# A hybrid encoder layer on one core: the feed-forward tiles lie 32 bytes further apart in SBUF

## The chip, the cores and the metric

The kernel runs on one NeuronCore of a Trainium2 chip. The metric is the device time of one execution in microseconds. Three executions of the kernel before took 3914.40, 3920.77 and 3924.82 us; the median, 3920.77 us, is the time before.

## The reference, cut to what matters

One layer: an input projection feeds a Hyena convolution and an RWKV-7 scan, their outputs are gated, joined and projected (`w_o`), normalised, and a SwiGLU feed-forward network follows. All data are float32; the sequence has 2048 rows of 1024 channels, the feed-forward network is 2816 wide.

```python
D_MODEL = 1024; SEQ = 2048
FFN_HIDDEN = ((8 * D_MODEL + 3 * 256 - 1) // (3 * 256)) * 256      # 2816
...
mix = (g_h * y_h + g_r * y_r) @ w_o
x = layer_norm(DN_ALPHA * x + mix, ln1_w, ln1_b)
ffn = (jax.nn.silu(x @ ffn_w_gate) * (x @ ffn_w_up)) @ ffn_w_down
return layer_norm(DN_ALPHA * x + ffn, ln2_w, ln2_b)
```

## The kernel before

Four stages follow one another in `build`: `project` (the input projection, with other work woven between its matmuls), `chain` and `hyena` (scan and convolution), `merge` (gates, `w_o`, first normalisation) and `ffn`. The first three take the span's first 2443 us or so, `ffn` the rest but its end.

**How a float32 product is made.** Every large operand is split into two tiles of type float32r: `hi`, a rounded copy that ScalarE casts (L196), and `lo`, what is left, which VectorE subtracts (L197). `mm3` (L199 to L203) then issues three matmuls, hi by hi (L201), and the two mixed ones (L202, L203), into one PSUM tile. In the feed-forward stage each has a moving operand of 512 columns and loads a new stationary operand of 128 columns (in a part of `merge` the moving operand has 256). The profile shows the load as an instruction of its own (PEld).

**The feed-forward stage.** `ffn` runs over two halves of 1024 tokens, and in each half over `NF` = 22 slices of 128 hidden channels. For each slice `weights` (L1803 to L1814) loads three pieces of 128 x 1024 (`fg`, `fu`, `fd`) into a raw tile and splits each into `fwh` and `fwl`, two buffers of each. For each of two blocks of 512 tokens the slice makes the gate `pg` and the up projection `pu` (8 x 3 matmuls each, stationary the weights, moving the transposed activations `fxh`, `fxl`), then `silu(pg) * pu`, split into the hidden tiles `hh` and `hl` (L1845). `down` multiplies those (stationary) with the `fd` tiles (moving) into `pd`, and VectorE adds `pd` to eight accumulators `acc0` to `acc7` (L1830). The down projection of one slice is put between the two blocks of the next, so that PE has work while ScalarE and VectorE finish the hidden tile. In all there are 2 x 22 x (96 + 48) = 6336 matmuls of 512 columns in the stage.

**Where the tiles lie.** Tiles come from pools; a pool sets its tags down one after the other, in the order in which they are first asked for, each at a multiple of 32 bytes. Beside `ffn`, the pool `mf` also serves `merge`: its 16 tiles `wo` (the split `w_o`, L1691) take the tags of the feed-forward weights and hidden tiles, so they lie at the same places. The first tile of `mf`, `leps` (L261), holds one constant but is 48 elements (192 bytes) wide. In the built program it starts at byte 83936 of a partition, and every tile of `mf` of 2 or 4 KB or more starts at a multiple of 256 plus 160. So do the activations of the first block (pool `xp1`) and the projection's weights (pool `wp`): **both operands of every float32r matmul of the kernel start at the same remainder, 160, modulo 256**, since the slices inside the tiles are whole multiples of 256 bytes. The raw tiles lie at remainders 96, 128 and 160.

**The order** of instructions follows the program text here, within each engine's queue; loads of weights are issued by SyncE, casts run on ScalarE, subtractions and sums on VectorE.

Of the kernel before, what the change touches and what calls it, by code (L numbers as in the profile page):

```python
# [188 lines left out]
class Layer:  # L189
# [38 lines left out]
    def build(self):  # L228
        tc, nc = self.tc, self.nc
        with tc.tile_pool(name="dr", bufs=1, space=DRAM) as dr, tc.tile_pool(name="keep", bufs=1, reuse_waits="tile") as keep:  # L230
            T = lambda n, s: dr.tile(s, F32, name=n)
            self.ident = self.load(keep, "c_ident")
            self.H3d = T("H3d", [P, 32, P])
            self.ud = T("ud", [27, P, L])
            self.gated = T("gated", [16, P, L])
            self.ABd = T("ABd", [2, NCH, P, HP, 256])
            self.Vd = T("Vd", [L, 512])
            self.gsd = T("gsd", [P, L])
            self.Yd = T("Yd", [NCH, P, 256])
            self.Hd = T("Hd", [2 * HT, 32, P, P])  # L240
            self.Nd, self.Wd = T("Nd", [2, P, 1024]), T("Wd", [2, P, 1024])
            self.yhd = T("yhd", [HT, P, L])
            self.bond = T("bond", [HP, P, L])
            self.yrd = T("yrd", [HP, P, L])
            self.x1d = T("x1d", [L, D])
            self.keep = keep

            self.Dk = keep.tile([P, 264], F32, name="Dk", tag="Dk")[:, 0:256].rearrange("p (d h c) -> p d h c", d=2, h=HP)
            with tc.tile_pool(name="xp1", bufs=1, reuse_waits="tile") as self.xp1, tc.tile_pool(name="fp", bufs=1, reuse_waits="tile") as self.fp:
                with tc.tile_pool(name="wp", bufs=1, reuse_waits="tile") as self.wp:  # L250
                    accp = tc.tile_pool(name="accp", bufs=2, space=PSUM, reuse_waits="tile")
                    self.accp = accp.__enter__()
                    self.cut, self.rush, self.stores = 1, 0, nc.scalar
                    self.project()
                    with tc.tile_pool(name="cm", bufs=1, reuse_waits="tile") as self.cm:
                        self.chain()
                        accp.__exit__(None, None, None)
                        self.hyena()
                    with tc.tile_pool(name="mf", bufs=1, reuse_waits="tile") as self.mf:

                        self.leps = self.mf.tile([P, 48], F32, name="leps")[:, 0:1]  # L261
                        for g in ("acc2", "acc3", "lw", "lb"):
                            self.mf.tile([P, D], F32, name=g, tag=g)
                        nc.vector.memset(self.leps, LN_EPS)
                        self.merge()
                        self.ffn()
# [1376 lines left out]
    def merge(self):  # L1643
        tc, nc, i, s = self.tc, self.nc, self.i, self.mf
        stt = nc.vector.scalar_tensor_tensor
        with tc.tile_pool(name="mgp", bufs=2, space=PSUM, reuse_waits="tile") as ps:
            ys = {"r": self.yr}
            wm = {"r": self.wr, "h": [s.tile([P, 8, 4, P], F32R, name=f"wh{n}", tag=f"fx{n}1") for n in "hl"]}
            for b in range(L // TB):
                tl = slice(TB * b, TB * b + TB)  # L1650
                rs = {}
                if b == 0:
                    rs = {dt: self.rs[dt // 4][:, dt % 4] for dt in range(7)}
                    y0, y2, w0 = self.early
                    self.branch_weights("h", 0, wm["h"], w0)
                    hl = [s.tile([P, 4, TB], F32R, name="y", tag=f"acc{2 + k}") for k in range(2)]
                    self.split(hl[0][:, 0:2], hl[1][:, 0:2], y0)
                    self.split(hl[0][:, 2], hl[1][:, 2], y2)
                    ys["h"] = [(hl[0][:, k], hl[1][:, k]) for k in range(3)] + [(self.yh[:, 0], self.yh[:, 1])]

                    def more(dt):
                        m = min(2, 8 - dt)
                        raw = self.wp.tile([P, 2, 4, P], F32, name="wr", tag="wl" if dt < 4 else "wh", bufs=2)[:, 0:m]
                        nc.sync.dma_start(raw, i["w_hy"][dt:dt + m].rearrange("c p k d -> p c k d"))
                        self.split(wm["h"][0][:, dt:dt + m], wm["h"][1][:, dt:dt + m], raw)

                    more(1)
                    more(3)
                mh, ml = ([s.tile([P, 4, TB], F32R, name="mx", tag=f"acc{4 + 2 * v + k}") for k in range(2)] for v in range(2))
                for dt in range(8):  # L1670
                    g = self.h512().rearrange("p (a b) -> p a b", b=TB)
                    part = [(0, "h", g[:, 0])]
                    if b == 0 and dt in (1, 3):
                        more(4 + dt)
                    if dt not in rs:
                        rs[dt] = g[:, 1]
                        part.insert(0, (1, "r", g[:, 1]))
                    for j, n, v in part:
                        self.gate(v, j, dt, tl)
                        p = ps.tile([P, TB], F32, name="pm", tag="pm" + n)  # L1680
                        self.joined(p, wm[n], ys[n], dt)
                        self.merged(v, v, p)
                    hi, lo = mh[dt // 4][:, dt % 4], ml[dt // 4][:, dt % 4]
                    o = g[:, 0]
                    nc.vector.tensor_tensor(out=o, in0=o, in1=rs[dt], op=ALU.add)
                    nc.scalar.activation(hi, o, AF.Copy, scale=0.5)
                    stt(out=lo, in0=o, scalar=0.5, in1=hi.bitcast(F32), op0=ALU.mult, op1=ALU.subtract)
                if b == 0:
                    self.ln_consts("ln1")
                    tags = [f"fw{v}{n}" for k in range(2) for n in ("fg", "fu", "fd") for v in "hl"] + ["hh", "hl"] * 2  # L1690
                    wo = [s.tile([P, D], F32R, name="wo", tag=g, bufs=2) for g in tags]  # L1691
                    for k in range(KT):
                        raw = self.raw()
                        nc.sync.dma_start(raw, i["w_o"][:, k])
                        self.split(wo[2 * k], wo[2 * k + 1], raw)
                if b + 1 < L // TB:
                    ys = {n: self.branch(n, b + 1) for n in "rh"}
                last = b == L // TB - 1
                if last:
                    self.x0 = []  # L1700
                    beside = self.turn_block(ps, ("pmr", "pmh"), 0, 0, self.x0)
                    next(beside)
                for t in range(2):
                    tk = 2 * b + t
                    tl = slice(P * t, P * t + P)
                    x = s.tile([P, D], F32, name="fx", tag="fx", bufs=FX)
                    nc.sync.dma_start(x, i["x"][P * tk:P * tk + P])
                    p = ps.tile([P, 2, 512], F32, name="po", tag="po")
                    for k in range(KT):
                        if last and t == 1:  # L1710
                            next(beside, None)
                        for n in range(2):
                            cl = slice(512 * n, 512 * n + 512)
                            self.mm3(p[:, n], mh[k // 4][:, k % 4, tl], ml[k // 4][:, k % 4, tl],
                                     wo[2 * k][:, cl], wo[2 * k + 1][:, cl], k == 0, k == KT - 1)
                    stt(out=x, in0=x, scalar=ALPHA, in1=p.rearrange("p a b -> p (a b)"), op0=ALU.mult, op1=ALU.add)
                    self.norm(s, x)
                    nc.sync.dma_start(self.x1d[P * tk:P * tk + P], x)
# [73 lines left out]
    def ffn(self):  # L1792
# [3 lines left out]
        with tc.tile_pool(name="ffp", bufs=2, space=PSUM, reuse_waits="tile") as ps:  # L1796
# [7 lines left out]
            def weights(f, spare=False):  # L1804
                w = {}
                for n in ("fg", "fu", "fd"):
                    raw = self.raw()
                    nc.sync.dma_start(raw, i[n][f].rearrange("p k c -> p (k c)") if n != "fd" else i[n][f])
                    t = "fu" if spare and n == "fd" else n
                    hi = s.tile([P, D], F32R, name="fwh", tag="fwh" + t, bufs=2)  # L1810
                    lo = s.tile([P, D], F32R, name="fwl", tag="fwl" + t, bufs=2)
                    self.split(hi, lo, raw)
                    w[n] = hi, lo
                return w  # L1814
# [24 lines left out]
            for half in range(2):  # L1839
                acc, nxt, pend = [], [], []  # L1840
                for f in range(NF):
                    if f:
                        w = weights(f, half and f == NF - 1)

                    hh, hl = (s.tile([P, 1024], F32R, name="h" + v, tag=f"fw{v}fg" if half and f == NF - 1 else "h" + v, bufs=2) for v in "hl")  # L1845
                    ready = f > 0 and not (half and f >= NF - 2)
                    for b in range(2):
                        xh, xl = xs[b]
# [44 lines left out]
```

## Time and profile before

| | |
|---|---|
| time before (median of 3; lowest, highest) | 3920.77 us (3914.40, 3924.82) |
| the profiled execution: its own time | 3916.3 us |
| its span, first to last instruction | 3913.2 us |
| around the span | 3.1 us |
| mean granted TensorE clock | 0.989 |
| busy: PE, PEld, DVE, ACT, POOL | 96%, 77%, 60%, 35%, 3% |

How to read it: PE is the matmul side of TensorE, PEld its weight loads (they run beside matmuls), DVE is VectorE, ACT ScalarE, POOL GpSimd, SP SyncE. The duration of one matmul (some 390 ns) is its way through the array, and successive matmuls overlap; what counts for the time is the distance from one matmul's start to the next one's, the **pitch**, which is read from a timeline or from a count of matmuls in a window. "fp32r" in a row is the split type.

### The profile page before, as it was taken

What the parts mean: (1) busy time and instruction counts of PE and PEld (TensorE: products, weight loads), DVE (VectorE), ACT (ScalarE), POOL (GpSimd) and SP (SyncE); (2) the same over time, 40 slices, a digit from 0 to 9 for tenths busy, and PEclk for the clock granted to TensorE, in tenths of its full rate; (3) what the DMA queues carried; (4) which work ended last, traced back from release to release, by engine and by line L of the source; (5) the groups of instructions that cost most, each with busy time, mean ns of one, the idle gap of its engine ahead of it and who ended that gap; (6) DMA issues with size and microseconds to landing.
All of it is one profiled execution on the core that took longest, in us unless ns stands there. A gap on an engine that the chain in (4) does not pass through costs nothing. (4 is left out here: it accounts for less than half of the span.)

```text
span 3913.2 us, 62098 instructions
## 1 busy us (share of the span) xinstructions
PE 3775.7 (96%) x24808; PEld 3001.6 (77%) x24808; DVE 2345.5 (60%) x3734; ACT 1366.3 (35%) x2583; POOL 127.8 (3%) x203
## 2 busy tenths in 40 slices
PE   8999999999999998999998999999999999999998
PEld 6776657788787887766657998788888878888887
DVE  4466885666667775667776556444444474444444
ACT  3355663333335655444444323211111141111113
POOL 0000001111010110000000000000000000000000
PEclk9999999999999999999999999999999999999999
DMA  4556878677777777756656334311111141111111
GB/s 138 175 167 175 219 216 254 194 227 212 208 221 229 219 221 224 203 151 175 172 153 196 117 115 137 134 49 49 49 49 49 49 146 59 49 49 49 49 49 43
DMA packets 430229, 551.48 MB, mean 141 GB/s; under 512 B 138019, under 2 KB 305451, under 8 KB 427187
## 3 DMA queue, kind: packets, MB, share of 16 engines
q1 hardware_dynamic: 364405, 459.37, 39.7%
q10 hardware_dynamic: 54528, 54.59, 4.6%
q0 software_dynamic: 11008, 33.57, 3.2%
q8 instruction: 195, 3.19, 0.4%
q14 instruction: 93, 0.76, 0.1%
HBM read 385.76 MB, written 144.70 MB: 136 GB/s over the span
## 5 line engine op out<-in xcount | busy, mean ns | idle before, releaser
L201 PE MATMUL acc<-xh,wh 128*128 128x512 f32 x1376 | 573.1, 417 | 11.7 <-ACT xh L196 8.8
L202 PE MATMUL acc<-xl,wh 128*128 128x512 f32 x1376 | 543.5, 395 | 3.8 <-DVE xl L197 3.8
L203 PE MATMUL acc<-xh,wl 128*128 128x512 f32 x1376 | 542.7, 394 | 0.5 <-DVE wl L197 0.5
L1830 DVE TENSOR_TENSOR acc<-pd,acc 128x1024 f32<-128x1024 f32 x320 | 387.4, 1221 | 68.6 <-PE pd L203 63.3
L196 ACT CAST fwh<-raw 128x1024 fp32r<-128x1024 f32 x132 | 138.9, 1052 | 702.3 <-PE pg L202 485.2
L201 PEld LDWEIGHTS acc<-xh,wh 128*128 128x128 f32 x1376 | 261.3, 190 | 120.2 <-issue 47.1
L1858 DVE TENSOR_TENSOR h<-pu,sg 128x512 f32<-128x512 f32 x88 | 60.9, 692 | 477.7 <-PE pu L203 470.6
L202 PEld LDWEIGHTS acc<-xl,wh 128*128 128x128 f32 x1376 | 261.9, 190 | 60.0 <-DVE xl L197 6.2
L203 PEld LDWEIGHTS acc<-xh,wl 128*128 128x128 f32 x1376 | 261.7, 190 | 58.6 <-DVE wl L197 1.7
L201 PE MATMUL pd<-fwh,hh 128*128 128x512 f32 x704 | 275.3, 391 | 1.6 <-DVE acc L1828 1.2
L201 PE MATMUL pu<-fxh,fwh 128*128 128x512 f32 x704 | 274.6, 390 | 0.4 <-ACT fxh L1744 0.4
L201 PE MATMUL pg<-fxh,fwh 128*128 128x512 f32 x704 | 274.7, 390 | 0.0
L203 PE MATMUL pd<-fwh,hl 128*128 128x512 f32 x704 | 274.6, 390 | 0.0
L202 PE MATMUL pd<-fwl,hh 128*128 128x512 f32 x704 | 274.6, 390 | 0.0
L203 PE MATMUL pg<-fxh,fwl 128*128 128x512 f32 x704 | 274.4, 390 | 0.0
L202 PE MATMUL pg<-fxl,fwh 128*128 128x512 f32 x704 | 274.4, 390 | 0.0
L203 PE MATMUL pu<-fxh,fwl 128*128 128x512 f32 x704 | 274.1, 389 | 0.0
L202 PE MATMUL pu<-fxl,fwh 128*128 128x512 f32 x704 | 274.0, 389 | 0.0
L197 DVE TENSOR_TENSOR fwl<-raw,fwh 128x1024 fp32r<-128x1024 f32 x132 | 161.2, 1222 | 167.3 <-ACT fwh L196 163.3
L197 DVE TENSOR_TENSOR wl<-wraw,wh 128x512 fp32r<-128x512 f32 (+1 forms) x217 | 169.5, 791 | 135.7 <-ACT wh L196 129.0
L196 ACT CAST wh<-wraw 128x512 fp32r<-128x512 f32 (+1 forms) x217 | 150.7, 703 | 223.8 <-PE acc L202 192.2
L201 PEld LDWEIGHTS pd<-fwh,hh 128*128 128x128 f32 x704 | 132.0, 188 | 40.3 <-DVE acc L1830 12.3
(298 smaller groups left out, 7195.5 us busy)
## 6 DMA issues: line engine op xcount, KB each, us to landing
wraw<-in_w_in SPq DMA_DIRECT2D x130, 512.0 KB
ABp<-ABd SPq DMA_DIRECT2D x64, 512.0 KB
raw<-in_fg SPq DMA_DIRECT2D x44, 512.0 KB
raw<-in_fu SPq DMA_DIRECT2D x44, 512.0 KB
raw<-in_fd SPq DMA_DIRECT2D x44, 512.0 KB
ud<-ev ACTq DMA_DIRECT2D x84, 256.0 KB
ABd<-AB SPq DMA_DIRECT2D x32, 512.0 KB
rg<-in_c_win POOLq DMA_DIRECT2D x64, 256.0 KB, 4.0
```

The costliest lines, as they stand in the source:

```text
L196: nc.scalar.copy(hi, src)
L197: nc.vector.tensor_tensor(out=lo, in0=src, in1=hi.bitcast(F32), op=ALU.subtract)
L201: mm(ps, ah, bh, start=start, stop=False)
L202: mm(ps, ah, bl, start=False, stop=False)
L203: mm(ps, al, bh, start=False, stop=stop)
L1830: tt(out=acc[t], in0=pf, in1=acc[t], op=ALU.add)
L1858: tt(out=h, in0=put, in1=sg, op=ALU.mult)
```

## The change

It makes five tile declarations wider, and uses the same number of elements of each as before: `leps` from 48 to 56 elements, and the tiles of the split `w_o`, of the split feed-forward weights and of the hidden activations from 1024 to 1032 elements, of which the first 1024 are used. So each such tile ends 32 bytes later, and everything behind it in the pool moves on.

```diff
-                        self.leps = self.mf.tile([P, 48], F32, name="leps")[:, 0:1]
+                        self.leps = self.mf.tile([P, 56], F32, name="leps")[:, 0:1]
...
-                    wo = [s.tile([P, D], F32R, name="wo", tag=g, bufs=2) for g in tags]
+                    wo = [s.tile([P, D + 8], F32R, name="wo", tag=g, bufs=2)[:, 0:D] for g in tags]
...
-                    hi = s.tile([P, D], F32R, name="fwh", tag="fwh" + t, bufs=2)
-                    lo = s.tile([P, D], F32R, name="fwl", tag="fwl" + t, bufs=2)
+                    hi = s.tile([P, D + 8], F32R, name="fwh", tag="fwh" + t, bufs=2)[:, 0:D]
+                    lo = s.tile([P, D + 8], F32R, name="fwl", tag="fwl" + t, bufs=2)[:, 0:D]
...
-                    hh, hl = (s.tile([P, 1024], F32R, name="h" + v, tag=f"fw{v}fg" if half and f == NF - 1 else "h" + v, bufs=2) for v in "hl")
+                    hh, hl = (s.tile([P, D + 8], F32R, name="h" + v, tag=f"fw{v}fg" if half and f == NF - 1 else "h" + v, bufs=2)[:, 0:1024] for v in "hl")
```

The instructions are the same in number, operation, operands and order on every engine, and each waits for the same. What differs is the start address of 676 tiles of `mf` (a buffer that is used again is counted each time). Start addresses modulo 256, from the two built programs:

| tiles | before | after |
|---|---|---|
| activations of the first block, `fxh`, `fxl` (pool `xp1`) | 160 | 160 |
| activations of the second block; weights `whh`, `whl` of `merge` | 160 | 192 |
| `acc2` to `acc7`, `h`, `lw`, `lb`, `mx` | 160 | 192 |
| `fwh` of `fg` and of `fd`, two buffers | 160, 160 | 192, 224 |
| `fwl` of `fg` and of `fd` | 160, 160 | 0, 32 |
| `fwh` of `fu` | 160, 160 | 64, 96 |
| `fwl` of `fu` | 160, 160 | 128, 160 |
| hidden `hh` | 160, 160 | 64, 96 |
| hidden `hl` | 160, 160 | 128, 160 |
| `wo`, 16 tiles | 160 each | each of the eight remainders twice |
| `fx`, `junk` | 160 | 192 |

The raw tiles, `acc0`, `acc1` and everything ahead of `merge` stay where they are. The last tile of the pool ends at byte 228288 of a partition (227744 before).

## The prediction

> **What bounds the kernel now.** I read the page first: its head, the busy shares and the chain that ended last.
>
> ```profile
> span 3913.2 us, 62098 instructions
> PE 3775.7 (96%) x24808; PEld 3001.6 (77%) x24808; DVE 2345.5 (60%) x3734; ACT 1366.3 (35%) x2583; POOL 127.8 (3%) x203
> PE 45%; DVE 2%; DMA 1%; ACT 1%; issue 0%; SPq 0%; DVEq 0%; ACTq 0%
> ```
>
> PE is busy 96% of the span, and no other engine holds more than 2% of the chain. The change touches `merge` and `ffn`, so I then asked for windows of that part: all engines over the stage, then PE alone in two quiet pieces and behind the last matmul.
>
> ```profile
> 2440.00:3902.00 1462.00, 1454.83 (x6438) 1194.45 (x6437) 724.85 (x732) 297.40 (x413) 0.00 (x0) 1.00 0.18 62
> ...
> 2700.00:3100.00 400.00, 400.00 (x1764) 1.00 0.15 49
> 3300.00:3700.00 400.00, 400.00 (x1763) 1.00 0.15 50
> 3902.00:3913.20 11.20, 0.00 (x0) 0.70 0.35 140
> ```
>
> In the first row the columns behind the length are busy time and count of PE, PEld, DVE, ACT and POOL, then granted clock, DMA share and GB/s; the others show PE alone. DVE works half of the stage (725 of 1462 us), ACT a fifth, DMA 18%. PE has no idle time in 2700 to 3100 and in 3300 to 3700: 400 us / 1763.5 matmuls is a pitch of **226.8 ns**. The stage's 6336 matmuls of 512 columns at that pitch are 1437 us; the other 25 us of the 1462 are transposes, the start and two changeovers. The stage is therefore a count times a pitch, and a change of addresses alone can matter only through the pitch, through 11 us of tail, or by making another engine late.
>
> **What the pitch is made of.** The timeline of `merge`, where the same product runs with 256 columns, gives a second point.
>
> ```profile
> 2087.94 0.28 PE L202 MATMUL pm<-y,whh 128*128 128x256 f32 x1
> ...
> 2088.90 0.28 PE L201 MATMUL pm<-y,whh 128*128 128x256 f32 x1
> ```
>
> Eight matmuls lie between these starts (by line: 202, 203, 201, and so on): 0.96 / 8 = 120 ns. So 256 columns more cost 226.8 - 120 = 106.8 ns, or 0.417 ns a column; 512 columns are 213.5 ns, and some **13 ns a matmul** are left over at either width. This rest is the only thing in the pitch that a collision of addresses could be hiding in. A float32 product, which reads its columns at half that speed, shows less of it:
>
> ```profile
> 1615.40 0.59 PE L1309 MATMUL pz<-Vf,Mc 128*128 128x512 f32 x1
> 1615.83 1.02 PE L1350 MATMUL pq<-rg,Mc 128*128 128x512 f32 x2
> 1616.68 1.02 PE L1351 MATMUL pq<-rg,Mc 128*128 128x512 f32 x2
> ```
>
> From 1615.40 to 1616.68 are three pitches of 0.427 us, and 1024 times 0.417 ns is the same 427 ns: a rest of some 2 ns at most. These operands start at remainders 224 and 96, not at one remainder. So either the rest of 13 ns belongs to the fast type, or it belongs to equal remainders; the profile does not hold the pair that would settle it, a float32r product with unequal ones.
>
> **The change, part by part.** *Instructions*: none is added, removed or moved, no operand and no wait differs, so nothing stands behind a new wait and no queue is passed. That term is 0. *DMA*: the raw tiles that the weights land in stay where they are: 0.
>
> *Matmuls*: 6336 in `ffn` and 768 of `w_o` in `merge`, 7104 in all, get a new pair of remainders or a new place; some 744 products of `merge` move with both operands by the same 32 bytes. Each nanosecond of mean pitch is worth 7.1 us, so 0.3% of the time (11.8 us, about what a measurement of this kernel can tell from no change) is 1.7 ns a matmul. Three observations speak for 0.
>
> First, the two streams do not keep step. A load of 64 stationary columns takes 140 ns, one of 128 takes 188:
>
> ```profile
> L847 PEld LDWEIGHTS pY<-SV,rg 128*64 128x64 f32 x1024 | 54.7, 140 | 0.0
> L201 PEld LDWEIGHTS pg<-fxh,fwh 128*128 128x128 f32 x704 | 132.5, 188 | 28.0 <-DVE fxl L1745 0.4
> ```
>
> That is 48 / 64 = 0.75 ns a column against 0.417 for the moving operand. While a load reads its 512 bytes (128 x 0.75 = 96 ns), the stream passes 96 / 0.417 = 230 columns or 920 bytes, and the distance between the two runs through 408 bytes, more than a whole turn of 256. Whatever remainder they start at, they meet at nearly every other. A start offset moves the moment of a meeting, not the number of meetings.
>
> Second, a shift in time is a shift of that distance, and the trace has some. Usually the next load starts with the matmul; at a changeover it comes late:
>
> ```profile
> 2487.69 0.39 PE L201 MATMUL pg<-fxh,fwh 128*128 128x512 f32 x1
> 2487.91 0.40 PE L201 MATMUL pd<-fwh,hh 128*128 128x512 f32 x1
> 2488.15 0.39 PE L202 MATMUL pd<-fwl,hh 128*128 128x512 f32 x1
> 2488.38 0.40 PE L203 MATMUL pd<-fwh,hl 128*128 128x512 f32 x1
> ...
> 2487.46 0.19 PEld L201 LDWEIGHTS pg<-fxh,fwh 128*128 128x128 f32 x1
> 2487.80 0.19 PEld L201 LDWEIGHTS pd<-fwh,hh 128*128 128x128 f32 x1
> ```
>
> The matmul of 2487.69 has a load beside it that starts 0.11 us late. By then the stream is some 110 / 0.417 = 264 columns or 1056 bytes in (the rows' 10 ns are 96 bytes, so which remainder the two then stand at is not known, only that it is hardly the same one as in step). Its pitch is 0.22 us, as ever. (The next pitch, 0.24, follows a load that came in time.)
>
> Third, the one pass in which the trace does have equal and unequal remainders is the transpose through the identity (remainder 128), with `y` at 128, `BK` at 64, `co` at 224, `fx` at 160:
>
> ```profile
> 1198.41 0.38 PE L882 MATMUL pgt<-k_c_ident,y 128*128 128x128 f32 x2
> 716.57 0.60 PE L790 MATMUL pT<-k_c_ident,BK 128*128 128x128 f32 x4
> 1579.45 0.93 PE L1282 MATMUL ph<-k_c_ident,co 128*128 128x128 f32 x7
> 3158.17 0.93 PE L1742 MATMUL pxt<-k_c_ident,fx 128*128 128x128 f32 x7
> ...
> L1742 PE MATMUL pxt<-k_c_ident,fx 128*128 128x128 f32 x128 | 18.6, 274 | 4.8 <-DMA fx<-x1d 2.3 <-DVE fxl L1745 1.9 <-DVE fwl L197 0.6
> ```
>
> With the 0.274 us of one (last row) taken off, the pitch is 0.106 for the equal pair (one step), and 0.109, 0.109 and 0.109 for the unequal ones: the same within the rows' rounding of 10 ns a step. These run at half speed, so they are weaker witnesses than the second.
>
> Bounds for this term: at best the rest falls from 13 ns to the 2 ns of the float32 rows, -11 ns or -78 us; at worst all pitches become the 0.235 us that the two behind 2487.91 show (0.47 / 2), +8 ns or +57 us. I take **0**, to which the three observations lie nearest, and keep both ends.
>
> *VectorE and ScalarE*: their tiles move as well. Both wait for PE in this stage:
>
> ```profile
> ACT fwh L196 <- PE pg L202: 485.2, 41, 13.3
> DVE h L1858 <- PE pu L203: 470.6, 85, 8.8
> ...
> L197 DVE TENSOR_TENSOR hl<-h,hh 128x512 fp32r<-128x512 f32 x88 | 60.1, 683 | 2.7 <-ACT hh L196 2.7
> L911 DVE TENSOR_TENSOR yo<-yo,bn 128x512 f32<-128x512 f32 x16 | 11.0, 689 | 3.4 <-ACT yo L893 3.3
> L485 DVE TENSOR_TENSOR sh<-u 128x512 f32<-128x512 f32 x60 | 40.7, 687 | 34.0 <-DMA u<-ud 33.7
> ```
>
> One VectorE form takes 683 ns on tiles at 160, 689 on tiles at 0 and 687 on tiles at other remainders: a spread of 1%, on an engine that is idle half of the time. PE's matmuls hide it; without that cover 1% of 725 us would be 7 us. In the tail, where nothing hides it, 1% of 11.2 us is 0.1 us. Does PE feel the others? In the two pieces of 400 us with DVE and ACT working beside it the pitch is as short as anywhere: 0. Sum: **0 us**.
>
> **What the pages say.** The Trainium skill, "SBUF — State Buffer", section "🔬 SBUF: two separate sides", has it that engines hinder one another only at the port shared by VectorE and GpSimd, which leaves addresses out; the sum by it is 0, and POOL's 0.00 us in the stage agrees. "TensorE: Matmul & The Clock Gate" of the Trainium skill, section "Back-to-back issue gap", gives N/2.4 + 2.5 ns, 216 ns at 512 columns. The 226.8 of this trace are 11 more, so by that page there would be 7104 x 11 = 78 us to win if equal remainders were what holds the fast type back; its section "Step-by-step: what each phase is for" speaks against that, since loads and streams have read ports of their own.
>
> **The rivals.** *Faster*: the rest of 13 ns is a collision of load and stream at equal remainders, and the change takes it away in 22 of 24 pairs of feed-forward tiles (of eight each in gate, up and down projection, two stay equal: 192 with 192 and 160 with 160). For it: the float32 rows, with unequal remainders and a rest of 2 ns. Against: the late load, the drift. In full 3920.8 - 78 x 22/24 = 3849 us; in part, anything from 3909.
>
> *Slower*: equal remainders are what keeps load and stream apart, since a load starts with its matmul and the same 32-byte slots are then read in a fixed order; unequal ones put both on one slot, and each such pair pays the 8 ns of the 0.235 us pitch. For it: a kernel with nearly all pitches at 226.8 and all remainders equal leaves room for only this. Against: the same drift. In full 3920.8 + 57 x 22/24 = 3973 us. It decides from 1.7 ns of mean pitch, when one pair in five pays.
>
> *It doesn't do what it says*: the addresses of the built program differ as stated, so this is out.
>
> **How the numbers follow.** The profiled execution took 3916.3 us, 3.1 of them around the span; with a sum of 0 it stays 3916.3. It lies 4.5 us under the median of the runs, 3920.8, which is what I forecast. Chances: no change 0.70, faster 0.17, slower 0.13; within 0.3% is 3909 to 3932.5. I let the rivals spread evenly over their partial forms. From 3878 to 3909 are 31 of the faster one's 60 us, 0.09; from 3932.5 to 3940 are 7.5 of the slower one's 40, 0.02. So 3878 to 3940 holds 0.70 + 0.09 + 0.02 = 0.81. The likeliest case alone spans 3909 to 3932.
>
> **What would show it.** Right: in windows without a stop PE again counts 1763 to 1764 matmuls in 400 us, whatever pair of remainders runs. Faster: more of them, up to 400 / 0.216 = 1852. Slower: down to 1702, and the timeline shows 0.23 to 0.24 for some pairs, always the same ones. A changed duration of VectorE's or ScalarE's rows with an unchanged count would leave the time alone. The forecast is wrong if the fast type, unlike the transposes, minds the start of its operands.

## The result, and the profile after

| | before | after |
|---|---|---|
| median of the runs | 3922.28 us (4 runs) | 3946.56 us (4 runs) |
| ratio | | 1.0068, 95% interval 1.0049 to 1.0087 |
| profiled execution: time, span | 3916.3, 3913.2 us | 3945.7, 3943.7 us |

The kernel became slower, by 0.7%. The head of the page, its busy shares and the chain of the kernel after:

```profile
span 3943.7 us, 62098 instructions
PE 3805.6 (96%) x24808; PEld 3001.2 (76%) x24808; DVE 2344.8 (59%) x3734; ACT 1366.1 (35%) x2583; POOL 127.4 (3%) x203
PE 53%; DMA 3%; DVE 2%; ACT 1%; issue 1%; SPq 0%; ACTq 0%; DVEq 0%
```

Counts are the same, DVE and ACT are as busy as they were to within 1 us, and PE is busy 29.9 us longer. The span grew by 30.5 us. The windows on PE alone, at the places shown of before, and the last 11.2 us with all engines (busy and count of PE, PEld, DVE, ACT, POOL; clock; DMA share; GB/s):

```profile
2700.00:3100.00 400.00, 400.00 (x1728) 1.00 0.15 48
3300.00:3700.00 400.00, 400.00 (x1728) 1.00 0.15 48
...
3932.50:3943.70 11.20, 0.00 (x0) 0.00 (x0) 6.20 (x8) 2.72 (x6) 0.00 (x0) 0.72 0.35 140
```

PE makes 1728 matmuls in 400 us without a gap, where it made 1764, at the same granted clock of 1.00: the pitch is 231.5 ns instead of 226.8. The 6336 matmuls of the feed-forward stage times 4.7 ns are 30 us, nearly the whole of the loss. From the start of the last matmul to the end of the span it took 11.9 us before and takes 11.6 us now, so the tail isn't longer. The groups of DVE show the durations of before for the sum into `acc`, 1221 ns, and for the split of the hidden tile, 683 ns before and 684 ns after (first row of before, then two of after):

```profile
L1830 DVE TENSOR_TENSOR acc<-pd,acc 128x1024 f32<-128x1024 f32 x320 | 387.4, 1221 | 68.6 <-PE pd L203 63.3
...
L1830 DVE TENSOR_TENSOR acc<-pd,acc 128x1024 f32<-128x1024 f32 x319 | 386.4, 1221 | 76.2 <-PE pd L203 74.0
L197 DVE TENSOR_TENSOR hl<-h,hh 128x512 fp32r<-128x512 f32 x88 | 60.2, 684 | 2.7 <-ACT hh L196 2.7
```

So the addresses act on the matmuls, and on all three products of the stage: from one matmul's start to the next, on the mean, 226.8, 226.7 and 227.5 ns for gate, up and down before, and 231.9, 231.4 and 231.8 after (steps over 260 ns, the few real stops, left out here and below).

### The profile page after: what moved, and what is told of

The parts are those of the page before. It is cut to its first block, busy times and chain, and to the rows that moved or that the text cites. A ratio compares the mean times of both kernels' runs of the same rounds, so it can differ in the third digit from the quotient of the medians.

```text
span 3943.7 us, 62098 instructions
## 1 busy us (share of the span) xinstructions
PE 3805.6 (96%) x24808; PEld 3001.2 (76%) x24808; DVE 2344.8 (59%) x3734; ACT 1366.1 (35%) x2583; POOL 127.4 (3%) x203
## 4 chain that ended last, share of the span: by engine, by line
PE 53%; DMA 3%; DVE 2%; ACT 1%; issue 1%; SPq 0%; ACTq 0%; DVEq 0%
PE pg L201 4%; PE pg L203 4%; PE pg L202 4%; PE pu L201 4%; PE pu L202 4%; PE pu L203 4%; PE pd L203 4%; PE pd L201 4%; PE pd L202 4%; PE pz L1309 2%; PE po L202 1%; PE po L203 1%; PE po L201 1%; PE pm L201 1%; PE pm L203 1%; PE pm L202 1%
## 5 line engine op out<-in xcount | busy, mean ns | idle before, releaser
L201 PE MATMUL acc<-xh,wh 128*128 128x512 f32 x1376 | 573.0, 416 | 14.4 <-ACT xh L196 8.5
L202 PE MATMUL acc<-xl,wh 128*128 128x512 f32 x1376 | 543.4, 395 | 4.6 <-DVE xl L197 4.5
L203 PE MATMUL acc<-xh,wl 128*128 128x512 f32 x1376 | 542.8, 394 | 0.8 <-DVE wl L197 0.8
L1830 DVE TENSOR_TENSOR acc<-pd,acc 128x1024 f32<-128x1024 f32 x320 | 387.6, 1221 | 76.2 <-PE pd L203 74.0
L201 PEld LDWEIGHTS acc<-xh,wh 128*128 128x128 f32 x1376 | 261.3, 190 | 118.9 <-issue 47.9
L202 PEld LDWEIGHTS acc<-xl,wh 128*128 128x128 f32 x1376 | 261.8, 190 | 65.4 <-issue 9.7
L203 PEld LDWEIGHTS acc<-xh,wl 128*128 128x128 f32 x1376 | 261.5, 190 | 59.1 <-DVE wl L197 2.1
L201 PE MATMUL pd<-fwh,hh 128*128 128x512 f32 x704 | 277.6, 394 | 1.2 <-DVE acc L1828 0.8
L203 PE MATMUL pd<-fwh,hl 128*128 128x512 f32 x704 | 278.7, 396 | 0.0
L201 PE MATMUL pu<-fxh,fwh 128*128 128x512 f32 x704 | 278.2, 395 | 0.4 <-ACT fxh L1744 0.4
L201 PE MATMUL pg<-fxh,fwh 128*128 128x512 f32 x704 | 278.0, 395 | 0.2 <-DVE fxl L1745 0.2
L203 PE MATMUL pg<-fxh,fwl 128*128 128x512 f32 x704 | 277.5, 394 | 0.0
L202 PE MATMUL pg<-fxl,fwh 128*128 128x512 f32 x704 | 276.9, 393 | 0.0
L203 PE MATMUL pu<-fxh,fwl 128*128 128x512 f32 x704 | 276.8, 393 | 0.0
L202 PE MATMUL pu<-fxl,fwh 128*128 128x512 f32 x704 | 276.8, 393 | 0.0
L202 PE MATMUL pd<-fwl,hh 128*128 128x512 f32 x704 | 276.5, 393 | 0.0
L197 DVE TENSOR_TENSOR fwl<-raw,fwh 128x1024 fp32r<-128x1024 f32 x132 | 161.2, 1221 | 171.0 <-ACT fwh L196 167.3
L201 PEld LDWEIGHTS pd<-fwh,hh 128*128 128x128 f32 x704 | 132.7, 189 | 38.4 <-issue 1.2
```

Source lines behind the costliest of these rows:

```text
L197: nc.vector.tensor_tensor(out=lo, in0=src, in1=hi.bitcast(F32), op=ALU.subtract)
L201: mm(ps, ah, bh, start=start, stop=False)
L202: mm(ps, ah, bl, start=False, stop=False)
L203: mm(ps, al, bh, start=False, stop=stop)
L1830: tt(out=acc[t], in0=pf, in1=acc[t], op=ALU.add)
```

## The experiments

Theory A: a matmul is slowed when the stationary load beside it and its own moving stream start at different remainders modulo 256. Theory B: remainder 160 is a good place and others are not. Theory C: what costs is that successive matmuls differ. Twelve kernels were run, two of them matmuls without the layer. The table gathers the other ten with the kernels before and after the change; mean pitch is over all products of the feed-forward stage.

| kernel | ratio to before, 95% | PE matmuls in 2700 to 3100 us | mean pitch, ns |
|---|---|---|---|
| before | 1 | 1764 | 227.0 |
| the change | 1.0068 (1.0049 to 1.0087) | 1728 | 231.7 |
| lead32 | 1.0032 (1.0016 to 1.0047) | 1745 | 229.4 |
| all128 | 0.9998 (0.9985 to 1.0010) | 1764 | 227.0 |
| d32_64_128 | 1.0113 (1.0084 to 1.0141) | 1719 | 232.9 |
| d224_160_32 | 1.0122 (1.0094 to 1.0151) | 1717 | 233.2 |
| x16_d96 | 1.0062 (1.0041 to 1.0082) | 1741 | 230.1 |
| lo_apart | 1.0100 (1.0079 to 1.0120) | 1727 | 231.8 |
| x_minus144 | 1.0026 (1.0012 to 1.0039) | 1750 | 228.8 |
| hidden_apart | 1.0026 (1.0013 to 1.0040) | 1751 | 228.7 |
| hidden_256 | 0.9994 (0.9981 to 1.0006) | 1763 | 227.2 |
| y_64_apart | 0.9984 (0.9972 to 0.9996) | 1764 | 227.1 |

### One remainder for nearly all, and another place for all

`lead32` takes one edit of the change, `all128` moves every tile behind `Dk`:

```diff
-                        self.leps = self.mf.tile([P, 48], F32, name="leps")[:, 0:1]
+                        self.leps = self.mf.tile([P, 56], F32, name="leps")[:, 0:1]
```

> Only leps is widened, so all of the pool mf moves by 32 bytes to remainder 192, weights, hidden tiles and second block alike; only the first block's activations stay at 160. In the changed kernel PE counts 1728 matmuls in 400 us (231.5 ns) against 1764 (226.8 ns) before. Theory A (a stationary load and the moving stream beside it collide when they start at different remainders): second block and down projection, where both are at 192, keep 226.7 ns; the gate and up products of the first block (a third of the stage, 160 against 192) cost some 5 ns more; about 1750 in 400 us, +10 us in all. Theory B (160 is a good place and others are not, whatever the partner): all products slower, about 1728, +25 us. Theory C (variety: each matmul starts its streams at another remainder than the one ahead of it): nothing varies within a run of matmuls, 1763, 0 us.

```diff
-            self.Dk = keep.tile([P, 264], F32, name="Dk", tag="Dk")[:, 0:256]...
+            self.Dk = keep.tile([P, 256], F32, name="Dk", tag="Dk")[:, 0:256]...
```

> Dk, one of the first tiles of the whole layout, is made 32 bytes narrower, so every later tile of the kernel moves down by 32 bytes: all float32r operands lie at remainder 128, none at 160. Theory A (difference of remainders): 1763 matmuls in 400 us, no change of time. Theory B (160 itself is good): 1728 or so, +25 us or more, since the input projection is touched too. Theory C: no change.

The timeline of PE in `lead32` (start, duration, line, tiles), first in the first block, whose activations alone stayed at 160, then in the second, where both operands lie at 192:

```profile
2801.54 0.40 PE L201 MATMUL pg<-fxh,fwh 128*128 128x512 f32 x1
...
2804.34 0.40 PE L201 MATMUL pg<-fxh,fwh 128*128 128x512 f32 x1
```

```profile
2825.71 0.39 PE L201 MATMUL pu<-fxh,fwh 128*128 128x512 f32 x1
...
2828.43 0.39 PE L201 MATMUL pu<-fxh,fwh 128*128 128x512 f32 x1
```

Twelve matmuls lie between the rows of each pair: 2.80 / 12 = 233 ns against 2.72 / 12 = 227. By products: 233.4 and 233.3 ns for the first block's gate and up, 227.0 and 226.7 for the second's. The place 192 is as good as 160, and in `all128`, where every float32r operand lies at 128, the time and the pitch are those of before. Theory B is out; for A the price is 6.6 ns at a difference of 32.

### A fixed difference for each product

Two kernels put unused gaps between the tiles, so that a product has one difference, the same for hi, lo and both buffers (gaps in elements of 4 bytes, by the place in `tags`):

```diff
+                    gaps = {0: 8, 2: 8, 4: 48, 12: 32}
...
+                        if k in gaps:
+                            s.tile([P, gaps[k]], F32, name=f"gap{k}", tag=f"gap{k}")
...
```

> Unused gaps between the tiles set one fixed difference of remainders for each of the three products, with hi, lo and both buffers alike: gate weights 32 bytes past the activations (192 against 160), up weights 64 past (224 against 160), hidden tiles 128 past the down weights (32 against 160). Theory A: each product has its own pitch, all above 226.7 ns, some 229 to 235; about 1728 in 400 us, +20 to +30 us. Theory C (variety from one matmul to the next): hi and lo lie at the same remainder, so nothing varies inside a product: 1760 or more, 0 to +3 us.

The other has `{0: 56, 2: 48, 4: 24, 12: 8}`.

> The same with other differences: gate weights 224 past (32 below) the activations, up weights 160 past, hidden tiles 32 past the down weights. Theory A: own pitches again, above 226.7 ns; if the sign or size of the difference matters, other ones than in the run with 32, 64 and 128; +15 to +30 us. Theory C: 1760 or more, 0 to +3 us.

Both are slower than the change itself, though nothing varies inside a product, so variety isn't needed. The pitches of gate, up and down were 233.0 (32), 233.3 (64) and 232.5 ns (128) in the first, 233.5 (224), 233.3 (160) and 232.8 (32) in the second: it costs 5 to 7 ns, and it hardly matters which of these differences it is. The totals came out above what was expected, 44 and 48 us.

### Matmuls alone

Is it PE by itself? A kernel of matmuls without the layer, with DVE, ACT and the DMAs at rest:

```python
for d in range(0, 256):              # stationary starts 4*d bytes past the moving operand
    for n in range(REP):
        o = d + 256 * (n % 2)
        mm(banks[n % 4], B[:, o:o + 128], A[:, 0:512], start=True, stop=True)
```

> Only matmuls, with nothing else at work: the layer is left out, and the output is whatever stands in PSUM. Eight matmuls for each start of the stationary operand, first 0 to 1020 bytes past the moving operand in steps of 4 (float32r, 512 columns), then 0 to 12032 in steps of 256, then 256 columns, float32 and bfloat16 in steps of 16 bytes, and at last both operands 32 bytes further on. Theory A: 226.7 ns at every whole multiple of 256 and 228 to 237 ns at the others, though ScalarE, VectorE and the DMAs stand still; with both operands moved by 32 bytes the curve shifts by 32. Theory that other engines' accesses are what collides: 226.7 ns at every offset. Open in both: whether some offset lies below 226.7 ns (the part above 213.3 ns would then be a collision as well), and whether the slower float32 stream and bfloat16 feel the offset at all.

Windows of PE in it: offsets of 4-byte steps, whole multiples of 256, float32 (two rows a product), bfloat16:

```profile
100.00:500.00 400.00, 400.00 (x1725) 1.00 0.00 1
530.00:570.00 40.00, 40.00 (x178) 1.00 0.00 1
630.00:830.00 200.00, 200.00 (x468) 1.00 0.00 0
861.00:911.00 50.00, 50.00 (x229) 1.00 0.00 1
```

Over a run through all offsets the count is close to that of the changed kernel, 1725 in 400 us against 1728, while nothing else works: **the loss comes from where PE's own two operands start**, not from other engines. How the two reads hinder each other isn't shown. All multiples of 256 from 256 to 12032 hold 226.7 ns (40 / 0.2267 = 176, and two at the edges). The curve repeats after 256 bytes, within 0.8 ns. With the moving operand 32 bytes further on, 226.6 ns stand where the stationary one is 32 bytes on too; the rest of the curve moves along only in part (at a difference of 240 bytes 226.6 instead of 228.8 ns, behind another offset). Float32 gave 429.2 ns and bfloat16 215.8 ns at each of 32 offsets: of the three types only float32r feels it.

### Which sequences are at rest

In the steps of 4 bytes no offset reached 226.7 ns within its eight matmuls, not even 0 (228.4 to 229.2 over the last five). So a second kernel of this kind holds each offset for 48 matmuls and then varies the sequence.

> Again only matmuls; the layer is left out, and the output is whatever stands in PSUM. First 48 matmuls for each offset of 0 to 252 bytes in steps of 4, then sequences that tell apart what has to be equal, each of 96 and each after 24 at rest (both operands at one remainder), then 256 columns in steps of 16 bytes, 48 each. Both operands 32 bytes on with each matmul (own pair equal, the next load unequal): 226.7 ns if the own pair counts, 230 or more if the load beside the stream does. Each moving operand where the next stationary lies (own pair unequal, load beside equal): the other way round. Only the moving, only the stationary moving on: 230 or more in both readings. One matmul in 24 at another remainder: one or two slow pitches if nothing is carried over; some ten, if a pitch depends on the one ahead, as the down projection of the run with 16 and 96 bytes suggests, which was slow at equal remainders where single gate products stand between. Half of 24 and 24: the same question. Offsets 144, 156, 228 and 252 hold 226.7 ns if the first run of this kind showed a property of the offset, not a chance of its start.

Start-to-start distances from its trace, in ns (the last 24 of 48 at one offset; otherwise all 96):

```
offsets 0, 120, 132, 144, 156, 228, 252            226.67
the other 57 of 64 offsets (4-byte steps)          228.3 to 236.7
both operands 32 bytes on, each matmul             234.2   (235, 234, 234, 234, 234, ...)
moving where the next stationary lies              230.8   (236, 226, 236, 226, ...)
only the moving / only the stationary moves on     234.1 / 234.1
one matmul in 24 elsewhere                         227.8   (228, 234, 234, 233, 231, 226, 227, ...)
24 here, 24 there                                  228.2   (236, 233, 236, 224, 231, 236, 228, 233, 230, 227, ...)
```

Windows of 18 to 20 us within three of these stretches: at rest, both operands moving on, and moving where the next stationary lies:

```profile
17.00:37.00 20.00, 20.00 (x90) 1.00 0.00 1
748.00:766.00 18.00, 18.00 (x78) 1.00 0.00 0
776.00:794.00 18.00, 18.00 (x80) 1.00 0.00 0
```

Both readings failed: neither an equal own pair nor an equal pair beside each other is enough, at 234 and 231 ns. And a pitch depends on those ahead of it: one odd matmul in 24 makes four slow pitches, more than the one or two and fewer than the ten that were expected, and behind one change of place (24 here, 24 there) nine pitches are off before 226.7 is reached again. So theory A is not enough, and C is right in part: equal remainders come to rest only in a sequence that **stays at one remainder** for some matmuls. Six other offsets of the 63 came to rest here too.

### The same in the kernel

`x16_d96` moves the second block's activations by 16 bytes, and the down weights and hidden tiles, together, by 96:

```diff
-            xs.extend(self.mf.tile([P, KT, 512], F32R, name="fx" + n, tag=f"fx{n}1") for n in "hl")
+            xs.extend(self.mf.tile([P, 4160], F32R, name="fx" + n, tag=f"fx{n}1")[:, 4:4100].rearrange("p (k c) -> p k c", k=KT) for n in "hl")
...
+                    gaps = {4: 24}
```

> The down weights and the hidden tiles lie 96 bytes past the rest, but at the same remainder (0), and the second block's activations 16 bytes past the gate and up weights (176 against 160); all else at 160 as before. Theory A: down projection and first block 226.7 ns; second block (a third of the stage) slower if 16 bytes are enough to matter, by up to 6.5 ns: 1745 matmuls in 400 us and +14 us at most, 1763 and 0 us if only steps of 32 count. Theory B (one good place): the down projection at remainder 0 is slower as well.

The loss was 24 us, more than the 14 expected at most. Its gate and up products took 228.3 and 226.8 ns in the first block (equal), 231.2 and 231.8 in the second: 16 bytes are enough. The down projection, equal at 0, took 231.1, which no rule about a single product gives. In this stage PE does not follow the program text to the letter: in most slices four gate products of the second block stand between the 36 down products ahead of it (12 down, 1 gate, 6, 2, 12, 1, 6). The timeline shows the down projection coming to rest and being thrown out:

```profile
2820.83 0.39 PE L203 MATMUL pd<-fwh,hl 128*128 128x512 f32 x1
2821.06 0.39 PE L201 MATMUL pd<-fwh,hh 128*128 128x512 f32 x1
2821.28 0.39 PE L202 MATMUL pd<-fwl,hh 128*128 128x512 f32 x1
2821.51 0.40 PE L203 MATMUL pd<-fwh,hl 128*128 128x512 f32 x1
2821.75 0.39 PE L201 MATMUL pg<-fxh,fwh 128*128 128x512 f32 x1
2821.98 0.40 PE L201 MATMUL pd<-fwh,hh 128*128 128x512 f32 x1
2822.22 0.40 PE L202 MATMUL pd<-fwl,hh 128*128 128x512 f32 x1
2822.45 0.39 PE L203 MATMUL pd<-fwh,hl 128*128 128x512 f32 x1
```

At 2821.06 the pitch is back at 0.22 and 0.23; then one gate matmul at another remainder comes between, with 0.24 ahead of it, and 0.24, 0.23 behind it.

`lo_apart` asked which pair of one matmul collides, with `gaps = {1: 16, 3: 112, 13: 8}`:

> Only some of the stationary tiles are set apart from the moving ones: of the gate weights lo by 64 bytes, of the up weights hi by 64, of the hidden tiles lo by 32. It tells which pair collides. If the load for the next matmul meets the stream that runs: in the gate product the matmul ahead of lo (L202) is slow and L201 and L203 stay at 226.7 ns; in the up product L201 and L203 are slow and L202 is not; in the down projection L202 alone. If a matmul's own pair counts: L203 slow in gate and down, L201 and L202 in up. Four of nine matmuls slow either way: about 4/9 of 44 us, +20 us.

A miss: by line (L201, L202, L203, steps within one product) gate took 230.4, 230.6, 232.9 ns, up 226.6, 235.7, 231.7, down 232.2, 236.6, 229.4. That is neither of the two patterns, and +39 us instead of +20. With four of nine matmuls apart the others don't come to rest either, which fits the sequences above.

`x_minus144` took an offset that had held 226.7 ns alone (the edit of `x16_d96`, without its gaps and with 28 in place of 4):

> Only the activations of the second block move, to remainder 16; everything else lies at 160, so the gate and up weights lie 144 bytes past them, the offset that held 226.7 ns in the run of matmuls alone. If what that run shows holds in the kernel: after some ten matmuls the second block's products run at 226.7 ns, the time is within 5 us of before, 1755 or more in 400 us. If only equal remainders are good in the kernel: 231 to 234 ns in a third of the stage, 1745, +12 us.

The second block did not come to rest; its timeline runs in a circle of three:

```profile
2800.16 0.40 PE L201 MATMUL pu<-fxh,fwh 128*128 128x512 f32 x1
2800.40 0.39 PE L202 MATMUL pu<-fxl,fwh 128*128 128x512 f32 x1
2800.62 0.39 PE L203 MATMUL pu<-fxh,fwl 128*128 128x512 f32 x1
2800.85 0.40 PE L201 MATMUL pu<-fxh,fwh 128*128 128x512 f32 x1
```

In the trace's nanoseconds these steps are 238, 225 and 231, over and over, 231.1 on the mean, and the time is 10 us longer. So an offset of 144 can hold 226.7 or 231 ns, by the sequence that it stands in; what in the sequence decides was not tested. Equal remainders came back to 226.7 in every run that kept to them for long enough; of the unequal ones tried in the layer none did.

### One part of the change, and its control

`hidden_apart` lengthens the hidden tiles alone by 32 bytes, `hidden_256` by 256:

```diff
-                    wo = [s.tile([P, D], F32R, name="wo", tag=g, bufs=2) for g in tags]
+                    wo = [s.tile([P, D + 8 * (g in ("hh", "hl"))], F32R, name="wo", tag=g, bufs=2)[:, 0:D] for g in tags]
...
-                    hh, hl = (s.tile([P, 1024], F32R, ...
+                    hh, hl = (s.tile([P, 1024 if half and f == NF - 1 else D + 8], F32R, ...
```

> One part of the change alone: the hidden tiles are 32 bytes longer, the weights and leps as before, so hh and hl lie at 160 and 224 in even slices, at 192 and 0 in odd ones. If a difference acts only on the products that have it: down projection at 230 to 234 ns, gate and up at 226.7, +9 to +14 us. If a disturbed sequence takes some matmuls to come to rest: also the first ten or so behind each down projection, +14 to +18 us.

> The same edit as in the run with the hidden tiles alone, but 256 bytes longer instead of 32, so that they move and all stay at remainder 160. If it is the remainder that costs: 1763 to 1764 matmuls in 400 us and no change of time (within 4 us), against +10 us with 32. If longer tiles or other addresses cost by themselves: +10 us again.

PE alone in 400 us, first with 32, then with 256:

```profile
2700.00:3100.00 400.00, 400.00 (x1751) 1.00 0.15 49
...
2700.00:3100.00 400.00, 400.00 (x1763) 1.00 0.15 49
```

With 32 the down projection took 231.3 ns, gate 227.8 and up 226.8: +10 us, the gate paying a little for what comes ahead of it. With 256 the same edit cost nothing that can be measured, 0.9994. It is the remainder, not the longer tiles.

### A faster kernel

In the run of sequences 256 columns behaved otherwise than 512: 120.0 ns at equal remainders, 113.3 at 64 and 192, 116.7 to 120 elsewhere. In `merge` the moving `y` of the Hyena branch lies in `acc2` and `acc3`:

```diff
-                        self.leps = self.mf.tile([P, 48], F32, name="leps")[:, 0:1]
+                        self.leps = self.mf.tile([P, 32], F32, name="leps")[:, 0:1]
                         for g in ("acc2", "acc3", "lw", "lb"):
                             self.mf.tile([P, D], F32, name=g, tag=g)
+                        self.mf.tile([P, 16], F32, name="gap")
```

> A try for a faster kernel. With 256 columns the run of matmuls alone held 113.3 ns where the stationary operand lies 64 bytes past the moving one, and 120 ns at equal remainders. In merge the moving tiles y of the Hyena branch (acc2, acc3, with lw and lb) move to remainder 96, the weights whh, whl and all else stay at 160. If the offset acts here as it does alone: the 744 products of 256 columns with whh and whl run at some 113 to 116 ns instead of 120, 3 to 5 us less in all, about 0.1% (at the limit of what five rounds can tell); the products with wh, in turn with them, may need some matmuls to come to rest again and give part of it back.

Products with `whh` and `whl`, then with `wh` and `wl`, in its timeline:

```profile
2144.78 0.28 PE L202 MATMUL pm<-y,whh 128*128 128x256 f32 x1
...
2145.35 0.28 PE L201 MATMUL pm<-y,wh 128*128 128x256 f32 x1
...
2145.70 0.28 PE L201 MATMUL pm<-y,wh 128*128 128x256 f32 x1
...
2146.65 0.28 PE L203 MATMUL pm<-y,wl 128*128 128x256 f32 x1
```

0.57 / 5 = 114 ns with the first, 0.95 / 8 = 119 with the second. On the mean 768 products went from 120.0 to 115.1 ns and 684 from 119.9 to 118.5, together 768 x 4.9 + 684 x 1.4 = 4.7 us. Measured 0.9984 (0.9972 to 0.9996), 1.6 to 11 us: a little faster than the kernel before, though the interval overlaps with those of `all128` and `hidden_256`, where every pair stays equal. Not all of the 4.7 us belongs to the 64 bytes. In `lead32` both operands lie at 192 for the first group (but for 24 products) and at 160 for the second, and the two took 119.0 and 118.5 ns. So the 1.4 ns of the second group come without an unequal pair, as soon as the two groups differ in place, and so perhaps does 1 ns of the first.

## Why the prediction was wrong, point by point

**What bounds the kernel** was read rightly: the stage is a count times a pitch, the tail did not grow, DVE and ACT kept their durations and stayed hidden, and no instruction was added. A nanosecond of pitch was said to be worth 7.1 us; 4.7 ns gave 30.5 us of span, not 33. From the first gate product to the last matmul 28.4 us were added, not 30, since the stage's few stops became some 1.5 us shorter. In `merge` the 768 products with `wo` went from 227.5 to 232.2 ns, which is 3.6 us; but the products of 256 columns, which the sum had at no change, went from 120.0 to 118.9 ns with `whh` and `whl` and from 119.9 to 118.3 ns with `wh` and `wl`, which takes 1.9 us back.

**The step that failed is the 0 taken for the pitch**, between bounds of -11 and +8 ns, and within it the first observation: "A start offset moves the moment of a meeting, not the number of meetings." In place of 0 the change showed 4.7 ns, and the runs of matmuls alone show 226.7 ns at an offset of 0 and 228 to 237 at 57 of 63 others. The argument took load and stream as two readers that pass each other freely, each at its own rate, and so left out that one matmul's pitch can change the meetings of those behind it. The sequences fit this: one change of place is felt for nine pitches. What happens when the two meet is not shown. Separate read ports for load and stream, which the prediction takes from the Trainium skill ("TensorE: Matmul & The Clock Gate", "Step-by-step: what each phase is for"), did not keep these 57 from being slower than 226.7 ns.

**The second observation** may have had a sign of this in its own rows. The matmul with the late load kept its pitch, and the next one's 0.24 was set aside, since its load "came in time". In the runs of matmuls alone the ones behind a disturbance pay too: 234 for a matmul at another place and 234, 233, 231 for the three behind it.

**The third observation**, the transposes, could not see it: they are float32 products, and float32 has 429.2 ns at every offset tried (at 512 columns). "Weaker witnesses" was too kind; a witness of another type was none.

**The rivals.** The slower one was what happened, at a chance of 0.13, and its sum of 57 x 22/24 = 52 us was too high for the change (27 us by the ratio), since not every matmul pays the 8 ns; with one fixed difference for each product it was 44 to 48 us. What it said of equal remainders holds in the main, but not its slots of 32 bytes: 4 bytes are enough. That equal remainders work by keeping load and stream apart stays a guess. The faster one, whose part above 213.5 ns would be a collision, is refuted for 512 columns: none of 64 offsets held less than 226.7, and the 2 ns of the float32 rows belong to that type. The Trainium skill ("TensorE: Matmul & The Clock Gate", "Back-to-back issue gap") gives 216 ns at 512 columns for an isolated matmul's gap, and 131 ns for a stream of loads and matmuls. The bfloat16 rows, each with a new load, took 215.8 ns and agree with the first figure; the float32r stream, at 226.7 ns or more, agrees with neither.

**The range** ended at 3940 because the slower rival's partial forms were spread evenly and only a fifth of a chance of 0.13 was taken in. The time lay 6.6 us beyond it.

What stays open: why the period is 256 bytes; why some 13 ns, the time of 32 columns, are lost even at rest; and why some offsets (120, 132, 144, 156, 228, 252) hold 226.7 ns alone.

## What to carry to other kernels

Where float32r matmuls bound the time, let the moving and the stationary tiles of all products that follow one another start at the same remainder modulo 256, and keep that through interleaved products too; at 512 columns it was worth 0.7 to 1.2% of this kernel. An argument that a resource's rate can't depend on a start needs a direct measurement when every instance in the trace has the same start: a run of some thousand matmuls gives the curve. And test a rule on the operand type that it is meant for.

## What the runs showed of the hardware that was not expected

- Float32r, 128 x 512 with a new stationary operand of 128 columns each time: 226.67 ns at equal remainders modulo 256, 232.1 ns on the mean of 64 offsets, 236.7 at the worst; 4 bytes of difference are enough (232.5).
- The same with 256 columns: 120.0 ns at equal remainders, 113.3 at 64 and 192 bytes after 48 matmuls at each (114 and 118 after eight, in the first run). What is best depends on the width.
- Float32 (429.2 ns a pass) and bfloat16 (215.8 ns), 512 columns: no dependence at any of 32 offsets.
- A pitch depends on the matmuls ahead: nine are off behind a change of place, and there are circles such as 238, 225, 231 that last through a whole product.
